# One more plain MLP chunk, wider right-operand steps, second-product loads in small pieces, its weight sums spread out, and the last steps row tile by row tile

## Chip, cores and metric

The kernel runs on 1 core of one Trainium2 chip. The metric is the device time of one execution in microseconds (us); the time before is the median of three runs. The profile is of one such execution.

## The reference

One decoder block on x of 1024 rows by 1024 columns, all in float32: sliding-window attention and a diagonal state-space branch beside each other, merged by gates, then a squared-ReLU MLP. The change touches the MLP alone:

```python
    h = rmsnorm(x, norm_mlp_pre[l])
    f = jnp.square(jax.nn.relu(h @ w_ff_in[l])) @ w_ff_out[l]   # 1024 -> 4096 -> 1024
    x = x + rmsnorm(f, norm_mlp_post[l])
```

## The kernel before

Every float32 operand of a matmul is split into a high part (rounded to the float32r type) by a ScalarE copy and a low part by a VectorE subtraction, and a product is three matmuls: high x high, high x low, low x high (`mm3`, lines 170 to 176). So the MLP keeps ScalarE and VectorE busy with splits while TensorE multiplies.

`mlp` (line 1322) makes the 4096 hidden columns in NC = 16 chunks of 256. The first N_WHOLE = 3 are plain: four products of 24 matmuls of 128x512, 96 a chunk, in halves over the rows (h = 0, 1) and the chunk's two column pieces (m = 0, 1). Chunks 0 and 1 run first their halves h = 0 and then their halves h = 1. The other chunks use Winograd's form of Strassen's scheme on a 2 x 2 blocking: seven products of 12 matmuls, 84 a chunk, with sums of blocks on both sides. The sums of the right operand, which serve all those chunks, are made by `ff1_rhs` (line 1260): T1, T2, T4 in tiles of their own, and T3 written over the block B[0, 1] of the normalised input. It is a generator in `self.side`, of which `tick` plays so many steps after each half product (`tick(9)` at 4 a step), and `drain` (line 190) plays what is left before the Winograd chunks begin. T4 is the third of three tiles from the pool `b16`, which holds seven buffers of 16 KB a partition; the buffer it gets is the one in which the second piece of weight chunk 1 is kept (`keep(self.big, (1,))`, line 217).

`units_ahead` (line 1196) feeds the Winograd chunks and the second product: a generator yields the operands one by one, `unit` (line 1185) emits the ScalarE copy at once and the VectorE low half a little later, and a ring of six buffers lets them be ahead of TensorE. `ff1_units` (line 1225) loads the raw weights of a chunk in two DMAs of 512 KB (line 1234) and makes its sums. `hid_out` (line 1310) makes four sums of a finished hidden chunk on VectorE and writes the chunk X and its sums S to `xd` in DRAM, 1 MB each (lines 1319 and 1320). All these DMAs are issued by SP's queue, which runs in order and waits at each issue until its data or its buffer are there.

The second product (`ff2`, line 1470; 4096 -> 1024) is one level of the same scheme: seven products M1, M2, M5, M6, M3, M7, M4 of 16 chunks by 4 row tiles by 3 matmuls = 192 matmuls. `ff2_units` (line 1436) yields for each chunk the left operand, read back from `xd` in pairs of chunks of 512 KB (line 1448, three buffers), and the right one, a chunk of a block of `w_ff_out` in `wb`. The blocks are loaded by `ff2_loads` (line 1425), one tile (1 MB for the first block, else 2 MB) at each of the first chunks of M1. Where the scheme wants a difference of blocks, `ff2_units` subtracts in place just ahead of the unit (lines 1457 and 1463): in M5, M6, M7 and M4. Between chunks `ff2` plays one of `steps`: copies and sums out of PSUM, in M7 the finished upper row tiles (`top`, `weigh`, `finish`: square on ScalarE with its sum, gain on POOL at line 1488, statistics, two scaled additions at line 1502, store), in M4 the preparation of the lower ones. The last four chunks of M4 run row tile by row tile; after each, `weigh` and, one tile later, `finish` follow.

What sets the order is the order of emission: each engine runs its instructions in the order in which this Python emits them, and semaphores hold them.

Of the kernel before, what the change touches and what calls it, by code (L numbers as in the profile page):

```python
# [9 lines left out]
F32 = mybir.dt.float32  # L10
# [15 lines left out]
N_WHOLE = 3  # L26
# [82 lines left out]
class Block:  # L109
# [1115 lines left out]
    def ff1_units(self, chunks):  # L1225
# [13 lines left out]
        for c in chunks:  # L1239
# [8 lines left out]
            yield self.unit(s[:, 1])  # L1248
            yield self.unit(A12)
            tt(s_[:, 0], A11, A21, ALU.subtract)  # L1250
            tt(s_[:, 1], A12, s[:, 1], ALU.subtract)
            yield self.unit(s[:, 0])
            held[0] -= 1
            load()
            yield self.unit(s_[:, 0])
            yield self.unit(s_[:, 1])
# [3 lines left out]
    def ff1_rhs(self):  # L1260
# [10 lines left out]
        def tt(o, x, y, op=ALU.subtract):  # L1271
            v.tensor_tensor(out=o, in0=x, in1=y, op=op)  # L1272
            return 4

        def put(o, k, t):
            nc.scalar.activation(out=o[0][:, k], in_=t, func=AF.Copy)
            late.append(lambda: tt(o[1][:, k], t, f(o[0][:, k])))
# [5 lines left out]
        def diff(k, x, y):  # L1283
            t, e = self.t([512]), self.t([512])
            yield tt(t, f(x[0][:, k]), f(y[0][:, k]))
            yield tt(e, f(x[1][:, k]), f(y[1][:, k]))
            yield tt(t, t, e, ALU.add)
            return t

        def less(k, x, y):  # L1290
            t = self.t([512])
            yield tt(t, f(x[0][:, k]), y)
            yield tt(t, t, f(x[1][:, k]), ALU.add)
            return t

        for k in range(4):
            t1 = yield from diff(k, B[0, 1], B[0, 0])
            put(T1, k, t1)
            t2 = yield from less(k, B[1, 1], t1)
            put(T2, k, t2)  # L1300
            yield from flush(1)
            t4 = yield from less(k, B[1, 0], t2)
            put(T4, k, t4)
            yield from flush(0)
        for k in range(4):
            t3 = yield from diff(k, B[1, 1], B[0, 1])
            put(B[0, 1], k, t3)
            yield from flush(0)
# [13 lines left out]
    def mlp(self):  # L1322
# [17 lines left out]
        for i in range(4):  # L1340
# [6 lines left out]
            for e in evacs[i]:  # L1347
                ev(ps[e], *divmod(e, 2), 0)
        self.side = [self.ff1_rhs()]
# [9 lines left out]
        for c in range(2, N_WHOLE):  # L1359
            X = self.r([4, 512])  # L1360
            pieces = [self.wq.get() for _ in range(2)]
            for h in (1, 0):
                for m in range(2):
                    for p in self.proj_halves(pieces[m], h, self.h2):
                        self.tick(9)
# [9 lines left out]
        for c in range(N_WHOLE, NC):  # L1375
# [24 lines left out]

            product("M1")
            late.append(lambda: nc.scalar.activation(out=m1, in_=ps["M1"], func=AF.Copy))
            product("M6")
            late.append(lambda: add(u, m1, ps["M6"]))
            product("M2")
            late.append(lambda: block(m1, ps["M2"], 0))
            product("M5")
            late.append(lambda: add(u5, u, ps["M5"]))
            product("M7")
            late.append(lambda: add(u7, u, ps["M7"]))  # L1410
            late.append(lambda: block(u7, ps["M5"], 3))
            product("M3")
            late.append(lambda: block(u5, ps["M3"], 2))
# [7 lines left out]
    FF2 = (("M1", (0, 0), (0, 0), None), ("M2", (0, 1), (1, 0), None), ("M5", (1, 0), (0, 0), (0, 1)),  # L1421
           ("M6", (1, 1), (0, 0), (1, 1)), ("M3", (1, 3), (1, 1), None), ("M7", (1, 2), (0, 1), (1, 1)),
           ("M4", (0, 3), (1, 0), (0, 0)))

    def ff2_loads(self):

        for j, n, pool, cs in ((0, 0, self.r, 4), (1, 0, self.big, 8), (0, 1, self.big, 8), (1, 1, self.big, 8)):
            self.wb[j, n] = []
            for c0 in range(0, NC, cs):
                t = pool([cs, 512], F32)  # L1430
                col = j * D + n * 512
# [243 lines left out]
```

## Time and profile before

| what | us |
|---|---|
| median of 3 runs | 1327.11 |
| lowest, highest run | 1324.92, 1328.24 |
| the profiled execution | 1324.95 |
| its span, first to last instruction | 1323.1 |
| TensorE busy in it | 1230.2 (93%) |
| VectorE, ScalarE, POOL busy | 888.8, 580.1, 124.6 |
| mean granted TensorE clock | 0.966 |

Times in the rows are microseconds from the span's start, durations of single instructions in a grouped row nanoseconds. PE is TensorE's matmul, PEld its weight load, DVE VectorE, ACT ScalarE, POOL GpSimd, SPq the queue that issues DMAs. L176 is line 176 of the kernel; a helper's line stands for all its callers, so the tile names tell them apart: `lo` and `hi` are the ring's unit buffers, `raw` the buffers of loads, `b`, `r`, `qp`, `t` tiles of the pools, `ps` PSUM. The part that the change touches runs from 638 us to the end.

### The profile page before, as it was taken

The page shows a single profiled execution, that of the slowest core. Times are in us where ns is not written, and L with a number is a line of the kernel's source. Part 1 is how long each engine was busy: PE and PEld are TensorE (multiplying, and loading weights), DVE is VectorE, ACT ScalarE, POOL GpSimd, SP SyncE. Part 2 cuts the span into 40 slices and gives each one's busy share as a digit, 9 for nine tenths or more (in the row PEclk, how much of TensorE's full clock was granted, in tenths as well). Part 3 has the DMA queues.
Part 4 walks back from the last instruction along what each step waited for, and adds up shares of the span by engine and source line. Part 5 has one row for each costly group of instructions (what it writes and reads, how often), then busy time and mean ns, then how long its engine had stood idle before and what let it go on. Part 6 is the DMA issues. An engine that isn't in the chain of part 4 may idle for free.

```text
span 1323.1 us, 15801 instructions
## 1 busy us (share of the span) xinstructions
PE 1230.2 (93%) x5784; PEld 1013.0 (77%) x5784; DVE 888.8 (67%) x1624; ACT 580.1 (44%) x1061; POOL 124.6 (9%) x78
## 2 busy tenths in 40 slices
PE   8999899999999999989966999999986999999795
PEld 7988788877889777768755888888864788887583
DVE  5776877645785566478597777777451476657987
ACT  4433566642114553554343555455341444444342
POOL 1000112200000033334000000000000000002212
PEclk8999899999999999999987999999998899999898
DMA  9322222298525574456042444543489222243342
GB/s 349 128 75 101 60 79 81 81 171 156 130 81 102 188 291 143 162 188 222 17 189 97 175 152 151 191 174 141 179 300 381 97 96 96 96 143 112 112 137 86
DMA packets 78749, 195.54 MB, mean 148 GB/s; under 512 B 6224, under 2 KB 23120, under 8 KB 73552
## 3 DMA queue, kind: packets, MB, share of 16 engines
q1 hardware_dynamic: 78672, 194.54, 45.1%
q8 instruction: 45, 0.74, 0.2%
q14 instruction: 32, 0.26, 0.1%
HBM read 135.30 MB, written 59.21 MB: 147 GB/s over the span
## 4 chain that ended last, share of the span: by engine, by line
PE 56%; DVE 20%; DMA 9%; ACT 8%; issue 5%; SPq 1%; POOL 1%; DVEq 0%; ACTq 0%
PE ps L175 17%; PE ps L174 17%; PE ps L176 17%; DMA raw<-xd 4%; DVE lo L158 2%; ACT r L535 2%; DVE b L164 2%; DVE t L1272 1%; DVE r L164 1%; ACT hi L156 1%; DVE lo L1193 1%; DMA raw<-in_wsb_dram 1%; DVE r L522 1%; PE ps L1157 1%; PE ps L1158 1%
## 5 line engine op out<-in xcount | busy, mean ns | idle before, releaser
L174 PE MATMUL ps<-b,hi 128*128 128x512 f32 x740 | 292.6, 395 | 1.7 <-ACT t L1039 1.3
L176 PE MATMUL ps<-b,lo 128*128 128x512 f32 x744 | 291.5, 392 | 0.9 <-DVE lo L1193 0.9
L175 PE MATMUL ps<-b,hi 128*128 128x512 f32 x740 | 289.6, 391 | 0.9 <-DVE b L164 0.9
L174 PE MATMUL ps<-lo,hi 128*128 128x512 f32 x440 | 177.1, 403 | 15.3 <-ACT lo L1192 15.3
L175 PE MATMUL ps<-lo,hi 128*128 128x512 f32 x440 | 178.0, 405 | 11.5 <-DVE lo L1193 11.4
L1193 DVE TENSOR_TENSOR hi<-raw,hi 128x512 fp32r<-128x512 f32 x128 | 90.0, 703 | 134.9 <-ACT hi L1192 134.9
L176 PE MATMUL ps<-lo,hi 128*128 128x512 f32 x440 | 175.5, 399 | 0.0
L1192 ACT ACTIVATE hi<-raw 128x512 fp32r<-128x512 f32 x128 | 80.6, 630 | 202.3 <-PE ps L176 116.2
L176 PEld LDWEIGHTS ps<-b,lo 128*128 128x128 f32 x744 | 140.7, 189 | 31.6 <-DVE lo L1193 1.6
L174 PEld LDWEIGHTS ps<-b,hi 128*128 128x128 f32 x740 | 139.6, 189 | 32.0 <-ACT t L1039 1.7
L175 PEld LDWEIGHTS ps<-b,hi 128*128 128x128 f32 x740 | 139.7, 189 | 30.0 <-DVE b L164 1.8
L158 DVE TENSOR_TENSOR lo<-raw,hi 128x1024 fp32r<-128x1024 f32 x66 | 87.9, 1336 | 82.5 <-ACT hi L156 82.1
L175 PEld LDWEIGHTS ps<-lo,hi 128*128 128x128 f32 x440 | 85.8, 195 | 35.3 <-DVE lo L1193 17.6
L174 PEld LDWEIGHTS ps<-lo,hi 128*128 128x128 f32 x440 | 85.3, 194 | 35.9 <-ACT lo L1192 17.8
L176 PEld LDWEIGHTS ps<-lo,hi 128*128 128x128 f32 x440 | 85.7, 195 | 17.7
L174 PE MATMUL ps<-b,lo 128*128 128x512 f32 x184 | 72.7, 395 | 22.7 <-ACT lo L1192 22.7
L156 ACT ACTIVATE hi<-raw 128x1024 fp32r<-128x1024 f32 x68 | 71.5, 1053 | 42.3 <-PE ps L1158 20.9
L175 PE MATMUL ps<-b,lo 128*128 128x512 f32 x184 | 72.4, 393 | 0.0
L176 PE MATMUL ps<-b,hi 128*128 128x512 f32 x180 | 70.0, 389 | 0.0
L1488 POOL TENSOR_TENSOR r<-r,qp 128x512 f32<-128x512 f32 x4 | 6.6, 1661 | 597.5 <-ACT t L1487 597.5
L1193 DVE TENSOR_TENSOR lo<-r,lo 128x512 fp32r<-128x512 f32 x73 | 50.1, 687 | 18.6 <-ACT lo L1192 18.6
L1192 ACT ACTIVATE lo<-r 128x512 fp32r<-128x512 f32 x73 | 45.4, 622 | 33.9 <-PE ps L176 32.8
(249 smaller groups left out, 2104.7 us busy)
## 6 DMA issues: line engine op xcount, KB each, us to landing
xd<-r SPq DMA_DIRECT2D x32, 1024.0 KB, 5.2
raw<-xd SPq DMA_DIRECT2D x56, 512.0 KB, 3.3
raw<-in_ff_dram SPq DMA_DIRECT2D x32, 512.0 KB, 5.7
raw<-in_win_dram SPq DMA_DIRECT2D x26, 512.0 KB, 4.5
raw<-in_wout_dram SPq DMA_DIRECT2D x24, 512.0 KB, 4.1
b<-in_ff_dram SPq DMA_DIRECT2D x6, 2048.0 KB, 16.2
r<-in_x_dram SPq DMA_DIRECT2D x14, 512.0 KB, 6.2
sd<-t SPq DMA_DIRECT2D x16, 256.0 KB, 2.0
```

The costliest lines, as they stand in the source:

```text
L156: nc.scalar.activation(out=hi, in_=src, func=AF.Copy)
L158: return (hi, lo), lambda: eng.tensor_tensor(out=lo, in0=src, in1=hi.bitcast(F32), op=ALU.subtract)
L164: (eng or nc.vector).tensor_tensor(out=lo, in0=src, in1=hi.bitcast(F32), op=ALU.subtract)
L174: self.nc.tensor.matmul(ps, lhsT=ah, rhs=bh, start=first and i == 0, stop=False)
L175: self.nc.tensor.matmul(ps, lhsT=ah, rhs=bl, start=False, stop=False)
L176: self.nc.tensor.matmul(ps, lhsT=al, rhs=bh, start=False, stop=last and i == n - 1)
L522: nc.vector.tensor_tensor_reduce(out=S[:, h - kv * G, 0:kk], in0=ps[:, gi, 0:kk], in1=self.bias[:, h, b0:256], op0=ALU.add, op1=ALU.max, s ...
L535: nc.scalar.activation(out=S[:, g, 0:kk], in_=S[:, g, 0:kk], func=AF.Exp, bias=nm[:, g:g + 1], accum_out=rs[:, g:g + 1])
L1157: nc.tensor.matmul(ac[c], lhsT=a, rhs=wl[:, cs], start=False, stop=False)
L1158: nc.tensor.matmul(ac[c], lhsT=b, rhs=wh[:, cs], start=False, stop=k == 7)
L1192: self.nc.scalar.activation(out=both[:, 0], in_=src, func=AF.Copy)
L1193: lo = lambda: self.nc.vector.tensor_tensor(out=both[:, 1], in0=src, in1=both[:, 0].bitcast(F32), op=ALU.subtract)
```

## The change

Constants: four plain chunks instead of three, and the last six chunks of M4 instead of four run row tile by row tile.

First product: the Winograd products come in the order M1, M2, M3, M5, M6, M7, M4, with u5 now M3 copied plus M5 and added to u later; the left sums of `ff1_units` stand behind the first unit. `ff1_rhs` works on 1024 columns at a time (28 steps instead of 56), its cost is 6.5 a step and a tick gives 11; T3's part waits until the last half product that reads B[0, 1] has been emitted.

Second product: `ff2_loads` goes. `ff2_jobs` gives each load (two chunks, 512 KB) and each weight difference a step, that is a chunk counted through the seven products. Eight loads of the first block come at steps 0, 0, 0, 2, 4, 6, 8, 10, the other 24 at 1.25 times their number; the differences at 24, 40, 52 and 66 plus the chunk. End: the gain is a VectorE step; sums, squares, gain, statistics and scaled additions become separate steps, `must` first and then `rest`, with two a chunk in M4; each half row is stored by itself (256 KB); of the last tiles' work the sum, square and gain of tile t stand ahead of the statistics of tile t - 1.

```diff
-N_WHOLE = 3
+N_WHOLE = 4
+TAIL = 6
...
+            yield self.unit(A11)
+            load()
             tt(s[:, 0], A21, A22, ALU.add)
             tt(s[:, 1], s[:, 0], A11, ALU.subtract)
-            yield self.unit(A11)
-            load()
...
-        for k in range(4):
-            t3 = yield from diff(k, B[1, 1], B[0, 1])
-            put(B[0, 1], k, t3)
+        while not self.b12_done:
+            yield "wait"
+        for ks in (slice(0, 2), slice(2, 4)):
+            t3 = yield from diff(ks, B[1, 1], B[0, 1])
+            put(B[0, 1], ks, t3)
             yield from flush(0)
...
             for p in self.proj_halves(first[i], 1, self.h2):
-                self.tick(9)
+                self.tick(11)
...
+        for i, (jn, c) in enumerate(itertools.product(((0, 0), (1, 0), (0, 1), (1, 1)), range(0, NC, 2))):
+            at(2 * i - 4 if i < 8 else 1.25 * i, functools.partial(load, *jn, c))
+        for c in range(NC):
+            at(24 + c, functools.partial(less, (0, 0), (0, 1), (0, 0), c))
+            at(40 + c, functools.partial(less, (0, 0), (1, 1), (0, 0), c))
+            at(52 + c, functools.partial(less, (0, 1), (1, 1), (0, 1), c))
+            at(66 + c, functools.partial(less, (1, 0), (1, 0), (0, 0), c))
...
-        load(2)
-        for name, _, at, less in self.FF2:
+        for i, (name, _, at) in enumerate(self.FF2):
             for c in range(NC):
-                w = self.wb[at][c]
+                for job in jobs.pop(i * NC + c, ()):
+                    job()
+                if i + c == 0:
+                    load(2)
...
-            nc.gpsimd.tensor_tensor(out=f, in0=f, in1=g[:, halves[n]], op=ALU.mult)
+        def gain(f, n):
+            v.tensor_tensor(out=f, in0=f, in1=g[:, halves[n]], op=ALU.mult)
...
+        def put(t, n, f, r1):
+            xx = x1[t][:, halves[n]]
+            v.scalar_tensor_tensor(out=xx, in0=f, scalar=r1, in1=xx, op0=ALU.mult, op1=ALU.add)
+            nc.sync.dma_start(out=self.out[0, t * P:(t + 1) * P, halves[n]], in_=xx)
...
+        def top(t):
+            f = C11[:, t], C12[:, t]
+            ss = self.small(3, "ss3")
+            for n in range(2):
+                squares(f[n], ss[:, n:n + 1])
+            gain(f[0], 0)
+            yield
+            gain(f[1], 1)
+            r1 = rstd(ss)
+            yield
+            for n in range(2):
+                put(t, n, f[n], r1)
+            if t == 0:
+                load_x1(3, self.q([D]))
+            yield
...
-            end = NC - 4 if name == "M4" else NC
+            end = NC - TAIL if name == "M4" else NC
...
-                next(self.wb_loads, None)
-                for _ in range(1 + (len(steps) > 12)):
-                    if steps:
-                        steps.pop(0)()
+                for _ in range(1 + (name == "M4")):
+                    if must:
+                        must.pop(0)()
+                    else:
+                        next(rest, None)
...
+            f, ss = U[:, 0, t], ss1[:, 2 * t:2 * t + 2]
+            tt(f, f, ps["M4"][t])
+            squares(f, ss[:, 0:1])
+            gain(f, 0)
             if prev:
                 prev()
-            tt(U[:, 0, t], U[:, 0, t], ps["M4"][t])
-            weigh(U[:, 0, t], 0, ss1[:, 2 * t:2 * t + 1])
-            prev = lambda t=t: finish(4 + t, (U[:, 0, t], U[:, 1, t]), ss1[:, 2 * t:2 * t + 2])
```

## Rows read from the trace of the kernel before

**Rows 1.** The page, busy time by engine: us (share of the span) xinstructions.

```profile
PE 1230.2 (93%) x5784; PEld 1013.0 (77%) x5784; DVE 888.8 (67%) x1624; ACT 580.1 (44%) x1061; POOL 124.6 (9%) x78
```

**Rows 2.** Windows: length, busy us (instructions) of each engine, granted clock, DMA share, GB/s.

```profile
682.50:705.50 23.00, 0.41 (x2) 0.00 (x0) 19.78 (x31) 7.14 (x13) 0.00 (x0) 0.61 0.44 160
705.50:712.00 6.50, 5.52 (x13) 3.94 (x14) 6.37 (x11) 2.92 (x6) 0.00 (x0) 0.55 0.08 27
712.00:956.70 244.70, 244.70 (x1080) 202.40 (x1078) 169.94 (x268) 116.73 (x197) 0.00 (x0) 1.00 0.46 163
956.70:986.80 30.10, 28.66 (x121) 22.21 (x120) 18.42 (x30) 14.70 (x26) 0.00 (x0) 1.00 0.79 258
986.80:1072.70 85.90, 70.55 (x267) 55.12 (x266) 32.31 (x51) 29.03 (x52) 0.00 (x0) 0.88 0.61 222
1203.20:1262.70 59.50, 49.43 (x194) 38.57 (x194) 52.04 (x89) 24.69 (x52) 13.44 (x8) 0.91 0.33 116
1289.90:1300.50 10.60, 9.08 (x37) 6.37 (x36) 9.82 (x13) 5.33 (x10) 2.48 (x2) 1.00 0.18 74
1308.90:1323.10 14.20, 0.13 (x1) 0.00 (x0) 8.13 (x20) 2.03 (x6) 2.52 (x2) 0.61 0.28 111
```

**Rows 3.** Waits of TensorE from 700 us on: total us, times, longest.

```profile
PE ps L174 <- ACT lo L1192: 38.0, 6, 22.7
PE ps L175 <- DVE lo L1193: 11.4, 10, 3.1
```

**Rows 4.** Timeline of ScalarE: start, us, instruction, [idle before it <-releaser].

```profile
661.08 0.63 ACT L1276 ACTIVATE b<-t 128x512 fp32r<-128x512 f32 x1 [13.59 <-PE ps L176]
```

**Rows 5.** Timelines of VectorE and TensorE at the first Winograd chunk.

```profile
705.63 0.68 DVE L1243 TENSOR_TENSOR r<-raw 128x512 f32<-128x512 f32 x1
706.35 0.69 DVE L1243 TENSOR_TENSOR r<-r,raw 128x512 f32<-128x512 f32 x1
706.96 0.68 DVE L1193 TENSOR_TENSOR lo<-raw,lo 128x512 fp32r<-128x512 f32 x1
...
707.70 0.80 PE L176 MATMUL ps<-b,lo 128*128 128x512 f32 x1 [0.92 <-DVE lo L1193]
```

**Rows 6.** SP's timeline at a chunk border; DMA issues of 732 to 735: KB, us to landing.

```profile
732.88 0.33 SPq L1319 DMA_DIRECT2D xd<-r  x1
734.20 7.94 SPq L1234 DMA_DIRECT2D raw<-in_ff_dram  x2
...
raw<-in_ff_dram SPq DMA_DIRECT2D x1, 512.0 KB, 7.3
```

**Rows 7.** Waits, 940 to 1030; DMA issues at 984; line 1448's landings, 1040 to 1110.

```profile
ACT hi L1192 <- DMA raw<-xd: 50.6, 5, 12.7
...
raw<-xd SPq DMA_DIRECT2D x1, 512.0 KB, 15.9
...
DMA to landing us min/median/max: 3.2/3.3/4.5
```

**Rows 8.** Timelines of VectorE and POOL in M7; waits of 1205 to 1250.

```profile
1208.50 1.78 DVE L1463 TENSOR_TENSOR b<-b,b 128x512 f32<-128x512 f32 x1
1209.69 1.74 POOL L1488 TENSOR_TENSOR t<-t,qp 128x512 f32<-128x512 f32 x1
...
ACT lo L1192 <- DVE b L1463: 24.1, 9, 3.7
```

**Rows 9.** VectorE's timeline at the last row tile; DMA issues of the whole span.

```profile
1314.74 0.68 DVE L1474 TENSOR_TENSOR b<-b,ps 128x512 f32<-128x512 f32 x1
1316.27 0.21 DVE L1493 TENSOR_SCALAR m<-mx 128x1 f32<-128x1 f32 x1 [0.85 <-ACT t L1487]
1318.01 1.41 DVE L1502 SCALAR_TENSOR_TENSOR b<-b,r,b 128x512 f32<-128x512 f32 x2
...
sd<-t SPq DMA_DIRECT2D x16, 256.0 KB, 2.0
...
out_dram<-b SPq DMA_DIRECT2D x4, 512.0 KB, 2.6
```

More of the change, by code (lines that the diff above doesn't have):

```diff
@@ L1436, in ff2_units @@
     def ff2_units(self):
         nc = self.nc
-        self.wb = {}
-        self.wb_loads = self.ff2_loads()
-        next(self.wb_loads)
-        raws = [(blk, c) for _, blk, _, _ in self.FF2 for c in range(0, NC, 2)]
+        self.wb, self.wb_tiles = {}, {}
+        jobs = self.ff2_jobs()
+        raws = [(blk, c) for _, blk, _ in self.FF2 for c in range(0, NC, 2)]
         loaded = []
@@ L1499, in finish @@
             v.tensor_tensor(out=r1, in0=r0, in1=e, op=ALU.mult)
-            for n in (1, 0):
-                ns = halves[n]
-                v.scalar_tensor_tensor(out=xx[:, ns], in0=f[n], scalar=r1, in1=xx[:, ns], op0=ALU.mult, op1=ALU.add)
-            nc.sync.dma_start(out=self.out[0, t * P:(t + 1) * P, :], in_=xx)
-        def top(t, ss):
-            f1 = self.t([512])
-            tt(f1, U[:, 0, t], U[:, 1, t])
-            tt(f1, f1, ps["M3"][t])
-            weigh(C11[:, t], 0, ss[:, 0:1])
-            weigh(f1, 1, ss[:, 1:2])
-            return lambda: finish(t, (C11[:, t], f1), ss)
+            return r1
+        def put(t, n, f, r1):
[17 more added lines that the diff above has]
+            yield
         ss1 = self.small(NH, "mx")
         ps = {}
-        for name, _, _, _ in self.FF2:
-            steps = list(late)
+        rest = iter(())
+        for name, _, _ in self.FF2:
+            must = list(late)
             late.clear()
-            each = lambda f: steps.extend(functools.partial(f, t) for t in range(4))
+            each = lambda f: must.extend(functools.partial(f, t) for t in range(4))
             if name == "M2":
@@ L1531, in ff2 @@
             if name == "M7":
-                for t in range(4):
-                    ss = self.small(3, "ss3")
-                    done = []
-                    steps += [lambda t=t, ss=ss, done=done: done.append(top(t, ss)), lambda done=done: done[0]()]
-                    if t == 0:
-                        steps.append(lambda: load_x1(3, self.q([D])))
+                C12 = self.big([4, 512], F32)
+                each(lambda t: tt(C12[:, t], U[:, 0, t], U[:, 1, t]))
+                each(lambda t: tt(C12[:, t], C12[:, t], ps["M3"][t]))
+                x1b = self.big([4, D], F32)
+                must.append(lambda: [load_x1(4 + t, x1b[:, t]) for t in range(4)])
+                rest = itertools.chain(*(top(t) for t in range(4)))
             if name == "M4":
-                x1b = self.big([4, D], F32)
                 each(lambda t: tt(U[:, 0, t], U[:, 0, t], ps["M7"][t]))
-                each(lambda t: tt(U[:, 1, t], U[:, 0, t], U[:, 1, t]))
-                each(lambda t: weigh(U[:, 1, t], 1, ss1[:, 2 * t + 1:2 * t + 2]))
-                each(lambda t: load_x1(4 + t, x1b[:, t]))
+                each(lambda t: (tt(U[:, 1, t], U[:, 0, t], U[:, 1, t]), squares(U[:, 1, t], ss1[:, 2 * t + 1:2 * t + 2])))
+                each(lambda t: gain(U[:, 1, t], 1))
             ps[name] = [self.ps() for _ in range(4)]
@@ L1556, in ff2 @@
                 make()
-                next(self.wb_loads, None)
-                for _ in range(1 + (len(steps) > 12)):
-                    if steps:
-                        steps.pop(0)()
-            for step in steps:
+                for _ in range(1 + (name == "M4")):
[3 more added lines that the diff above has]
+                        next(rest, None)
+            for step in must:
                 step()
+        for _ in rest:
+            pass
         aw = [(c, get(), get()) for c in range(end, NC)]
```

117 lines of the change are left out of this document (64 added, 53 removed).

## The prediction

> **What bounds the kernel now.** TensorE is busy for 93% of the span [rows 1], so I looked first for the stretches where it is not, and asked for the busy times of the MLP in windows cut at those places [rows 2]. The reader is to see one clean window and several broken ones. From 712 to 956.7 us, 1080 matmuls take 244.7 us: one each 0.2266 us at full clock, nothing lost. That price times the matmuls that a window must run, taken from its length, gives what the window loses (the counts in the rows include one to three that straddle an edge; I use the program's numbers, 192 for a product of the second matrix):
> - 682.5 to 712: 29.5 us for 13 matmuls, **26.5 lost**.
> - 956.7 to 986.8: 30.1 for 120, **2.9 lost**; 986.8 to 1072.7: 85.9 for 264, **26.1 lost**.
> - 1203.2 to 1262.7: 59.5 for 192, **16.0 lost**.
> - 1289.9 (end of chunk 9 of the last product M4) to the end at 1323.1: **33.2 us**, of which 14.2 follow the last matmul.
>
> The granted clock is below 1.00 in all of these but the first 30 us of the second product and the stretch before 1308.9 (0.55 to 0.91), and the losses contain that. Next the waits of TensorE [rows 3]: 38.0 us on ScalarE's unit copies (22.7 once, 15.3 in five others) and 11.4 on VectorE's low halves. What stood behind each comes from the timelines and the DMA views [rows 4 to 9], in the parts below.
>
> **The extra plain chunk and the wide steps.** The 26.5 us are `drain()`: VectorE still works at `ff1_rhs` when the three plain chunks end. It was late because ScalarE's copy into T4 sat 13.59 us until 661.1 [rows 4]: T4's buffer is the one that holds a weight piece until then. The fourth plain chunk is 96 matmuls in place of 84, so 12 x 0.2266 = **+2.7 us** of TensorE, and 21.8 us of cover. VectorE owes 28 wide steps; two narrow ones start 0.61 apart [rows 5], so a wide one is about 1.2. The ninth stands behind T4's copy, so some nine are done by 661; 19 x 1.2 = 23 plus three `hid_out` (2.5 each) and three weight splits (1.2 each) makes 34 us, due by 704.3, 43 us later. So the steps hide, even though T3's eight wait for `b12_done` and have the last half chunk (10.9 us) for about 10 us of work.
>
> But a new thing is late: **the first raw weights of the Winograd chunks**. `ff1_units` issues them only after `hid_out(3)` on SP, whose first issue waits for the last matmul's two ScalarE passes. Count from the last plain matmul: 1.7 us to that issue (0.4 of matmul end, two passes of 0.63 as in [rows 4]); the same three issues stand at a chunk border, where the raw follows the first xd write by 1.32 us and lands 7.3 us later behind 2 MB of writes [rows 6]. So A11 lands at 10.3, is copied by 10.9, the first two matmuls go. VectorE's two sums now stand ahead of A11's low half and need the second raw, issued 1.2 us after the first: they start at 11.5, and sum, sum, low half took 2.0 us (705.63 to 707.64 [rows 5]); the third matmul goes at 13.5, as it went at 707.70 before. Less 0.7 of useful matmuls, plus some 2 us of low clock as the rows after 705.5 show, **14.9 lost instead of 26.5: -11.6**. Bounds: 5 if the loads came at once, 26.5 if nothing were covered.
>
> **Order inside the Winograd chunks** (M1, M2, M3, M5, M6, M7, M4): one more ScalarE copy, the same VectorE adds. TensorE loses nothing there now and VectorE is busy 170 of 245 us, so 0.
>
> **Second product's loads.** The 26.1 us are four waits of ScalarE on raw xd reads: 50.6 us in five waits, 12.7 the longest (that one sits ahead of the product) [rows 7]. These 512 KB reads landed after 15.9 us, against 3.3 in undisturbed products [rows 7], because 15 of the 16 MB of `wb` went out within nine chunks. Now 13 pieces of 0.5 MB and 8 raws go out in M1: 11 MB in 43.5 us is 253 GB/s, no more than the 258 moved up to 986.8, with 2.9 lost, and the 222 after it, over twice the time [rows 2], and each piece is issued four chunks (10.9 us) before its use. On SP each stands behind a raw whose buffer VectorE must free, at most a chunk or so; that leaves twice the 3.3 us. **26.1 goes to about 0.5: -25.6.** Ahead of the first raw, three pieces (1.5 MB) replace one of 1 MB: at 258 GB/s 0.5 MB is 2.0 us; the ring of units is empty there, so it shows, less a little that VectorE's own backlog hides: **+1.6**. The bounds are 0 and +3, and 0 to 12 for loads that remain late.
>
> **Weight sums spread out, gains on VectorE.** In M7 VectorE was busy 52 of 59.5 us: low halves, 16 sums, the four finished row tiles, all in that product. POOL's gain of 1.74 us stretched a VectorE step from 0.68 to 1.78, and ScalarE waited 24.1 us for the sums [rows 8]. Now M7's 16 sums run in M6 and M3 and M4's 16 in M3 (two of them in M7), and the gain is one VectorE step of 0.68. The busiest earlier product, M6, then holds 32 low halves and 20 sums, 52 x 0.61 = 32 us of 43.5; M7 holds 32 low halves, 2 sums, 8 adds and 2 1/3 row tiles (some 6 us each): 42 x 0.61 + 14 = 40. A gain waits for ScalarE's square, itself behind the unit copies; that delays VectorE by at most one chunk of the three that the ring holds. **16.0 goes to 0.5: -15.5**; bounds -16 and -8.
>
> **The last steps.** Call E the end of chunk 9 of M4. Before, E to end was 33.2. The row tiles that are left (5 of 12 steps) fall in chunks 6 to 8: gains 3 x 0.7, two statistics chains of 1.74 [rows 9] with ScalarE's root behind unit copies, four puts of 0.7. Chained through, VectorE is free for chunk 10's low halves only at E+1 and for the six last chunks' at E+8.6, so row tile 0 ends at E+9.3, not E+4.1. Then per tile: add to statistics 1.53 [rows 9], in which the gain waits for the square, gain 0.65, chain without POOL about 1.45, puts 1.35: 5.0 us against 4.1 of matmuls, first two tiles without backlog. Ends: E+11.6, 18.5, 23.6, 28.6, last chain and puts 31.4. Then 3.7 us from 1319.4 to the span's end, less 0.6 as a 256 KB store lands in 2.0 and a 512 KB one in 2.6 [rows 9]: 34.5, with 0.7 for a possible low clock 35.2: **+2.0**. So row-tile order gains nothing: VectorE sets this end before and after. Bounds -3 and +9 (the tiles at half clock).
>
> **Sum**, against the profiled execution (1324.95, its span 1323.1 and 1.85 around it): -11.6 + 2.7 - 25.6 + 1.6 - 15.5 + 2.0 = -46.4, so 1278.5. The median of the three runs lies 2.2 above the profiled one; I carry most of that and say **1280**.
>
> **Rivals.**
> - The raws arrive earlier or VectorE's order doesn't matter: only 5 lost at the border, 1270. For: an undisturbed read lands in 3.3 [rows 7]. Against: SP is in order, and the 2 MB lie ahead. Chance 0.15.
> - What is covered is only partly so: leftover `ff1_rhs` (up to +11.6), M1's loads half late (+12), or the last tiles at half clock (+7); one of them gives 1287 to 1296. For: VectorE idles until 661 whatever is emitted, and the last product is crowded. Against: the slack counted above. That the extra chunk covers nothing at all is 1292, within this. Chance 0.23.
> - Slower than before: small pieces don't overlap, each holds the path for its whole landing. By their steps M1 and M2 carry 13 pieces and 8 raws each, M5 6 and 8: 21 x 3.3 [rows 7] = 69 us twice and 14 x 3.3 = 46, in place of 43.5 each: +54, 1334. It decides from 2.1 us of path for each transfer in M1. Against: at 258 GB/s [rows 2] a piece is 2.0 us of path, and two or more were in flight then. Chance 0.04.
> - The rule behind that rival: the Trainium skill, "DMA: Bandwidth & Descriptors", section Bandwidth, asks for transfers of 1 MiB and more, as smaller ones waste the path, and so speaks against cutting 2 MB loads into 0.5 MB. By that rule the time is nearer to 1334, by the rows 1280: a 0.5 MB read took 3.3 us by itself and 15.9 behind two 2 MB loads [rows 7], so here it is the large ones that hold the path, and I give the rule no more than that chance.
>
> **How the numbers follow.** Forecast 0.58 (1272 to 1287), earlier border 0.15, partial cover 0.23, slower 0.04. The range 1264 to 1295 leaves out about two in ten. About 0.3%, 4 us, is what a measurement of this kernel can tell from no change. Only the serial rival, and a little of mishaps that I don't see, reaches it: faster 0.94, same 0.02, slower 0.04.
>
> **What would show it.** In the changed profile: a hole of 10 to 14 us after the last plain matmul that ends with a raw's landing, with `ff1_rhs` done before it (right), or with VectorE in `ff1_rhs` (wrong); no ScalarE wait on raw<-xd above 1 us in M1's second half; raws landing under 8 us; M7 at 43.5 to 45 us; VectorE late at the last six chunks, then its chain of adds and puts to the end. The prediction is wrong if the border closes in 5 us, or if M5 and M6 show new waits on `wb` loads.

## The result, and the profile after

The changed kernel takes 1278.38 us (median of four runs, 1276.39 to 1281.95) against 1326.01 (1322.52 to 1328.24) for the kernel before in the same comparison: a ratio of 0.965, 95% interval 0.961 to 0.968. Forecast were 1280 and 1264 to 1295. The profiled execution took 1276.67 us with a span of 1274.9; the one of before had 1324.95 and 1323.1, so the spans differ by 48.2.

The page's busy times, which answer to [rows 1]: TensorE does 12 matmuls more and is 95% busy instead of 93%, VectorE has 28 instructions fewer.

```profile
PE 1216.6 (95%) x5796; PEld 1007.3 (79%) x5796; DVE 871.9 (68%) x1596; ACT 581.1 (46%) x1059; POOL 99.8 (8%) x62
```

The windows of the changed kernel that answer to [rows 2], with the same columns (start and end, length, busy time and count of PE, PEld, DVE, ACT and POOL, granted clock, DMA share, GB/s): the last plain chunks, the border, the Winograd chunks, M1 and M2, M7, the end up to about the last matmuls, and what follows them.

```profile
638.00:703.70 65.70, 65.45 (x287) 53.97 (x288) 47.12 (x48) 28.81 (x42) 0.00 (x0) 1.00 0.26 104
703.70:724.00 20.30, 7.43 (x22) 5.15 (x21) 8.81 (x13) 6.14 (x10) 0.00 (x0) 0.66 0.58 207
724.00:948.10 224.10, 224.10 (x990) 185.34 (x988) 153.43 (x242) 110.64 (x188) 0.00 (x0) 1.00 0.45 162
949.30:1040.00 90.70, 89.57 (x385) 73.17 (x386) 55.92 (x89) 44.78 (x79) 0.00 (x0) 0.98 0.79 268
1170.50:1214.10 43.60, 43.60 (x194) 36.08 (x194) 30.76 (x58) 21.51 (x42) 0.00 (x0) 1.00 0.48 169
1241.30:1261.40 20.10, 17.35 (x70) 12.49 (x69) 14.55 (x29) 6.20 (x16) 0.00 (x0) 1.00 0.14 53
1261.40:1274.90 13.50, 0.87 (x4) 0.38 (x2) 8.23 (x25) 1.57 (x5) 0.00 (x0) 0.62 0.32 117
```

The reader is to see that M7 has become a clean window (43.6 us for 192 matmuls, clock 1.00) where it took 59.5, that M1 and M2 together now need 90.7 us where they took 30.1 + 85.9, and that the one long broken window left ahead of the end is the 20.3 us at the border.

Below, "lost" is the time from one matmul's start to the next over 0.227 us, added up over a stretch of the trace. E is, as in the prediction, the end of chunk 9 of M4. One term of the sum is not lost time: the 12 matmuls.

| stretch | lost before | lost after | change | forecast |
|---|---|---|---|---|
| border before the Winograd chunks | 26.3 | 15.7 | -10.7 | -11.6 |
| 12 more matmuls | | | +2.7 | +2.7 |
| M1 and M2, with the first units of M1 | 29.0 | 4.9 | -24.2 | -25.6 + 1.6 |
| M7 | 15.9 | 0.0 | -15.9 | -15.5 |
| E to the end of the span (all of it) | 33.2 | 33.6 | +0.4 | +2.0 |
| up to the start of the part that the change touches | | | -0.5 | 0 |
| sum | | | -48.2 | -46.4 |

M5, M6 and M3 lose nothing in either kernel. The last line but one is not the change's doing: in the executions told of below this part (it begins with the halves h = 1 of chunks 0 and 1, at 638.5 before and 638.0 after) starts anywhere from 636.8 to 641.5 us, whatever was edited. So single executions are compared here by what a stretch loses, and not by their totals alone.

**The border.** The timeline of TensorE, VectorE, ScalarE and SP in the changed kernel (start, duration, instruction, idle time before it and what ended it), and the landing of the loads that SP issues from 706.51 on (count, KB, median us from issue to landing):

```profile
703.71 0.39 PE L177 MATMUL ps<-b,lo 128*128 128x512 f32 x1
715.49 0.79 PE L175 MATMUL ps<-b,lo 128*128 128x512 f32 x1 [11.39 <-ACT lo L1193]
718.19 0.80 PE L177 MATMUL ps<-b,lo 128*128 128x512 f32 x1 [1.48 <-DVE lo L1194]
...
706.37 1.23 DVE L1273 TENSOR_TENSOR b<-r,b 128x1024 fp32r<-128x1024 f32 x1 [0.25 <-ACT b L1277]
716.11 0.69 DVE L1244 TENSOR_TENSOR r<-raw 128x512 f32<-128x512 f32 x1 [8.52 <-DMA raw<-in_ff_dram]
...
714.81 0.63 ACT L1193 ACTIVATE lo<-raw 128x512 fp32r<-128x512 f32 x1 [8.47 <-DMA raw<-in_ff_dram]
...
705.42 0.32 SPq L1322 DMA_DIRECT2D xd<-r  x1
706.14 0.32 SPq L1323 DMA_DIRECT2D xd<-r  x1
706.51 3.79 SPq L1235 DMA_DIRECT2D raw<-in_ff_dram  x3
...
raw<-in_ff_dram SPq DMA_DIRECT2D x3, 512.0 KB, 8.3
```

The last step of `ff1_rhs` (L1273) is done at 707.6, and then VectorE and ScalarE both stand still for 8.5 us until the raw weights land: what the prediction called the new late thing.

**The end.** VectorE's timeline of the last row tiles, which answers to [rows 9]: the four additions of a finished tile into the sum (L1497), one gain between them, and the last pair of scaled additions.

```profile
1250.02 0.69 DVE L1497 TENSOR_TENSOR b<-b,ps 128x512 f32<-128x512 f32 x1 [0.83 <-PE ps L177]
...
1258.98 0.68 DVE L1497 TENSOR_TENSOR b<-b,ps 128x512 f32<-128x512 f32 x1
1260.45 0.69 DVE L1512 TENSOR_TENSOR b<-b,qp 128x512 f32<-128x512 f32 x1 [0.79 <-ACT t L1509]
1263.86 0.68 DVE L1497 TENSOR_TENSOR b<-b,ps 128x512 f32<-128x512 f32 x1
...
1270.26 1.41 DVE L1527 SCALAR_TENSOR_TENSOR b<-b,r,b 128x512 f32<-128x512 f32 x2
```

### The profile page after: what moved, and what is told of

It reads as the page before. It is cut to its first block, busy times and chain, and to the rows that moved or that the text cites. A ratio compares the mean times of both kernels' runs of the same rounds, so it can differ in the third digit from the quotient of the medians.

```text
span 1274.9 us, 15769 instructions
## 1 busy us (share of the span) xinstructions
PE 1216.6 (95%) x5796; PEld 1007.3 (79%) x5796; DVE 871.9 (68%) x1596; ACT 581.1 (46%) x1059; POOL 99.8 (8%) x62
## 4 chain that ended last, share of the span: by engine, by line
PE 66%; DVE 16%; ACT 8%; DMA 5%; issue 4%; SPq 1%; POOL 0%; DVEq 0%; ACTq 0%
PE ps L175 20%; PE ps L176 20%; PE ps L177 20%; DVE lo L159 2%; ACT r L536 2%; DVE b L165 2%; DVE r L165 1%; DVE r L523 1%; ACT hi L157 1%; DMA raw<-in_ff_dram 1%; PE ps L1158 1%; PE ps L1159 1%; PE ps L1157 1%; DMA raw<-in_win_dram 1%; DMA r<-ud 1%
## 5 line engine op out<-in xcount | busy, mean ns | idle before, releaser
L175 PE MATMUL ps<-b,hi 128*128 128x512 f32 x760 | 300.1, 395 | 1.7 <-ACT t L1040 1.3
L177 PE MATMUL ps<-b,lo 128*128 128x512 f32 x760 | 297.4, 391 | 1.5 <-DVE lo L1194 1.5
L176 PE MATMUL ps<-b,hi 128*128 128x512 f32 x760 | 296.9, 391 | 0.9 <-DVE b L165 0.9
L176 PE MATMUL ps<-hi,lo 128*128 128x512 f32 x432 | 169.2, 392 | 2.9 <-DVE hi L1194 2.9
L175 PE MATMUL ps<-hi,lo 128*128 128x512 f32 x432 | 168.9, 391 | 1.1 <-ACT hi L1193 1.1
L175 PEld LDWEIGHTS ps<-b,hi 128*128 128x128 f32 x760 | 143.2, 188 | 32.9 <-ACT t L1040 1.8
L177 PE MATMUL ps<-hi,lo 128*128 128x512 f32 x432 | 168.9, 391 | 0.0
L176 PEld LDWEIGHTS ps<-b,hi 128*128 128x128 f32 x760 | 143.3, 189 | 30.6 <-DVE b L165 1.8
L1193 ACT ACTIVATE lo<-raw 128x512 fp32r<-128x512 f32 x126 | 79.5, 631 | 183.1 <-PE ps L177 152.2
L1194 DVE TENSOR_TENSOR lo<-raw,lo 128x512 fp32r<-128x512 f32 x126 | 87.1, 691 | 89.5 <-ACT lo L1193 89.2
L176 PEld LDWEIGHTS ps<-hi,lo 128*128 128x128 f32 x432 | 81.5, 189 | 21.5 <-DVE hi L1194 4.8
L175 PEld LDWEIGHTS ps<-hi,lo 128*128 128x128 f32 x432 | 81.5, 189 | 18.5 <-ACT hi L1193 1.5
L177 PEld LDWEIGHTS ps<-hi,lo 128*128 128x128 f32 x432 | 81.4, 188 | 17.0
L175 PE MATMUL ps<-b,lo 128*128 128x512 f32 x168 | 66.5, 396 | 11.4 <-ACT lo L1193 11.4
L176 PE MATMUL ps<-b,lo 128*128 128x512 f32 x168 | 66.1, 394 | 0.0
L177 PE MATMUL ps<-b,hi 128*128 128x512 f32 x168 | 65.4, 389 | 0.0
L1194 DVE TENSOR_TENSOR hi<-r,hi 128x512 fp32r<-128x512 f32 x72 | 49.5, 687 | 22.4 <-ACT hi L1193 22.4
L1193 ACT ACTIVATE hi<-r 128x512 fp32r<-128x512 f32 x72 | 44.7, 621 | 35.5 <-PE ps L177 35.5
L1158 PE MATMUL ps<-lo,b 128*128 128x512 f32 x128 | 51.0, 399 | 5.5 <-DVE lo L159 5.3
```

The costliest lines, as they stand in the source:

```text
L175: self.nc.tensor.matmul(ps, lhsT=ah, rhs=bh, start=first and i == 0, stop=False)
L176: self.nc.tensor.matmul(ps, lhsT=ah, rhs=bl, start=False, stop=False)
L177: self.nc.tensor.matmul(ps, lhsT=al, rhs=bh, start=False, stop=last and i == n - 1)
L1158: nc.tensor.matmul(ac[c], lhsT=a, rhs=wl[:, cs], start=False, stop=False)
L1193: self.nc.scalar.activation(out=both[:, 0], in_=src, func=AF.Copy)
L1194: lo = lambda: self.nc.vector.tensor_tensor(out=both[:, 1], in0=src, in1=both[:, 0].bitcast(F32), op=ALU.subtract)
```

## Experiments

The labels with r are edits of the changed kernel, those with b of the kernel before. Where no ratio is given, the number is of one execution.

**The first raw loads ahead of the last stores.** Theory: the hole at the border is SP's order alone. Rival: VectorE's or ScalarE's backlog sets it.

```diff
         load()
+        yield
         for c in chunks:
...
+        units = self.ff1_units(range(N_WHOLE, NC))
         for c in range(2, N_WHOLE):
             X = self.r([4, 512])
             pieces = [self.wq.get() for _ in range(2)]
+            if c == N_WHOLE - 1:
+                next(units)
...
-        make, get = self.units_ahead(itertools.chain(self.ff1_units(range(N_WHOLE, NC)), self.ff2_units()))
+        make, get = self.units_ahead(itertools.chain(units, self.ff2_units()))
```

> The changed kernel with one thing moved: the first three raw loads of the Winograd chunks are issued when the fourth plain chunk begins, ahead of its hid_out on SP's queue. Theory (the hole of 11.8 us at the border is the landing of these loads, held by SP's order): the hole ends when ScalarE has finished the last evacuation and T3's copy, 3.3 us after the last plain matmul, and the third matmul goes some 5.8 us after it instead of 14.5; the border loses 6 to 8 us instead of 15.7, the execution takes 8 to 10 us less than the changed kernel's 1276.7, so about 1268. Rival (the hole is VectorE's and ScalarE's remaining steps of ff1_rhs, and the loads only end last by a little): 0 to 3 us less.

Measured: 1270.09 us (1267.83 to 1271.35) against 1323.69 for the kernel before beside it, ratio 0.960 (0.958 to 0.962). TensorE at the border:

```profile
702.83 0.39 PE L177 MATMUL ps<-b,lo 128*128 128x512 f32 x1
706.03 0.50 PE L175 MATMUL ps<-b,lo 128*128 128x512 f32 x1 [2.81 <-ACT lo L1193]
708.71 0.79 PE L177 MATMUL ps<-b,lo 128*128 128x512 f32 x1 [1.94 <-DVE lo L1194]
```

The hole is 3.2 us from start to start instead of 11.8, the third matmul comes 5.9 us after the last plain one instead of 14.5, and the border loses 7.9 instead of 15.7. SP now issues these loads at 684.8 us, 18 us before the last plain matmul, so the order on SP was the cause. ScalarE's two passes over the last product and T3's copy (703.3 to 705.5) hold what is left of the hole, and VectorE's last step of `ff1_rhs` with the two left sums what is left ahead of the third matmul.

**Three plain chunks again.** How much is the extra chunk worth in the changed kernel?

```diff
-N_WHOLE = 4
+N_WHOLE = 3
```

> The changed kernel with three plain chunks again, all else kept. Theory (with the raw loads behind hid_out, the border's hole is the larger of leftover ff1_rhs and the loads): VectorE ends hid_out(2) about 9 us after the last plain matmul, the loads land some 8 us later, the border loses about 21 us instead of 15.7, and 12 matmuls (2.7 us) are saved: 2 to 4 us more than the changed kernel, about 1279. Rival (the extra chunk is what takes the old loss away): the loss of 26 us is back, 8 us more.

Measured: 1278.69 us, 2.0 above the profiled execution of the changed kernel. SP's timeline at the border, and the waits between 681 and 702 us (total, times, longest):

```profile
685.24 0.32 SPq L1322 DMA_DIRECT2D xd<-r  x1
690.34 0.32 SPq L1323 DMA_DIRECT2D xd<-r  x1
690.71 2.46 SPq L1235 DMA_DIRECT2D raw<-in_ff_dram  x3
...
PE ps L175 <- ACT lo L1193: 15.4, 1, 15.4
ACT lo L1193 <- DMA raw<-in_ff_dram: 8.2, 1, 8.2
```

Without the extra chunk the hole is 15.8 us and the border loses 20.0, 4.3 more than with it; the 12 matmuls cost 2.7 of that. The sums that the second store writes stand behind steps of `ff1_rhs` on VectorE (four wide ones from 682.95 on) and end at 690.3, so that store is 5 us behind the first one, not 0.7 as in the changed kernel, and the raw loads behind it on SP with it. So, as the kernel stands, the chunk brings some 2 us (4.3 - 2.7 at the border, 0.5 in M1): most of its cover goes to waiting for a load that nothing but its place in the queue holds back.

With three plain chunks as before, this border still loses 6.3 less than in the kernel before. VectorE ends `ff1_rhs` 9.6 us after the last plain matmul (691.5 against 681.9), before 23.2 (705.7 against 682.5). VectorE's idle time around T4's copy, in the kernel before and in this run, shows where it gained:

```profile
662.90 0.69 DVE L1314 TENSOR_TENSOR r<-r 128x512 f32<-128x512 f32 x1 [12.13 <-ACT r L1331]
...
661.63 1.23 DVE L1273 TENSOR_TENSOR b<-r,b 128x1024 fp32r<-128x1024 f32 x1 [4.51 <-ACT b L1277]
```

Ahead of that idle time VectorE has done nine steps of `ff1_rhs` in both, but here each is twice as wide.

**Narrow steps again.** Are the wide steps of `ff1_rhs` worth anything?

```diff
-            return 6.5
+            return 4
...
-        for ks in (slice(0, 2), slice(2, 4)):
+        for ks in (slice(k, k + 1) for k in range(4)):
...
-                self.tick(11)
+                self.tick(9)
```

> The changed kernel with the steps of ff1_rhs 512 columns wide again (56 steps at 4, a tick gives 9), the wait for the last reader of B[0, 1] kept. Seven of T3's 16 steps are then left for the drain, some 6 us of VectorE after the last plain matmul, while the raw loads land 11 us after it: by my account the border loses 15.7 us as with wide steps, the execution changes by less than 2 us. Rival (the wide steps are what lets ff1_rhs end in time): the border loses 3 us more or above.

Measured: 1275.87 us; the border loses 15.5 against 15.7. They are worth nothing that shows here, since `ff1_rhs` ends before the raw weights land either way: with narrow steps its last one ends at 711.4 us and the first Winograd matmul starts at 714.6.

This and the run before take out the chunk and the wide steps one at a time, each with the other in place, and in a kernel whose border waits for the loads either way. No run takes out both, nor either of them once the loads are moved. There the wide steps could show: `ff1_rhs` ends 3.9 us after the last plain matmul with them (707.6 against 703.7) and 8.4 without (711.4 against 702.9). So 2 us and nothing are what each is worth beside the other, and not what they would be worth alone.

**Large loads at the spread times, and small loads early.** The prediction set the small pieces against a rule of the Trainium skill that asks for large ones. The change did two things at once, size and time, and these two runs take them apart. First, 2 MB (for the first block 1 MB) in one transfer at the step of its first piece; then the 0.5 MB pieces at about the times of the kernel before.

```diff
         def load(j, n, c):
...
-            self.nc.sync.dma_start(out=t[:, i:i + 2], in_=self.I["ff2"][c:c + 2, :, col:col + 512].rearrange("c p x -> p c x"))
+                col = j * D + n * 512
+                self.nc.sync.dma_start(out=t, in_=self.I["ff2"][c:c + cs, :, col:col + 512].rearrange("c p x -> p c x"))
```

> The changed kernel, but each tile of the second product's right operand loaded whole (1 or 2 MB in one DMA) at the step of its first piece, so large loads spread out as the small ones are. Theory A (what cost 26 us before was that nearly all loads went out within nine chunks): no change beyond 2 us, M1 and M2 of the second product lose about 5 us as now. Theory B (large transfers hold the path whenever they run, small pieces are the cure): waits on raw reads come back at each of the seven 2 MB or 1 MB loads, 10 to 25 us more.

```diff
-            at(2 * i - 4 if i < 8 else 1.25 * i, functools.partial(load, *jn, c))
+            at((0, 0, 3, 3, 4, 4, 5, 5)[i] if i < 8 else 6 + (i - 8) // 4, functools.partial(load, *jn, c))
```

> The changed kernel with its small pieces of 0.5 MB, but issued as early as before: the first block's at steps 0 to 5, the other 24 at four a step from step 6 to 11. Theory A (timing is the cause): the path is again full for some 40 us, raw reads land after 10 us or more, 15 to 25 us more than the changed kernel. Theory B (size is the cause): no change beyond 2 us.

Measured: 1277.28 us with large loads spread out, 1301.36 with small loads early. M1 and M2 lose 5.8 in the first, 27.8 in the second, 4.9 in the changed kernel and 29.0 before. The windows of M1 and M2 with large loads, then with small early ones, and of each the landings of its DMAs (count, KB, us from issue) from 949 to 1000 and from 960 to 1010; last the wait of ScalarE in the second (total, times, longest):

```profile
949.80:1040.50 90.70, 89.69 (x385) 72.96 (x386) 55.91 (x89) 44.79 (x79) 0.00 (x0) 0.98 0.72 261
...
raw<-xd SPq DMA_DIRECT2D x9, 512.0 KB, 5.0
b<-in_ff_dram SPq DMA_DIRECT2D x2, 2048.0 KB, 10.0
```

```profile
949.90:1064.70 114.80, 97.43 (x385) 75.94 (x384) 55.09 (x88) 44.23 (x79) 0.00 (x0) 0.93 0.66 234
...
b<-in_ff_dram SPq DMA_DIRECT2D x24, 512.0 KB, 10.8
raw<-xd SPq DMA_DIRECT2D x7, 512.0 KB, 10.8
...
ACT lo L1193 <- DMA raw<-xd: 49.1, 5, 12.1
```

The early small pieces bring back the picture of [rows 7] almost to the number (50.6 us in five waits there, 49.1 in five here), the spread large ones don't. The time of issue is the cause; the size is not, as it moves M1 by 0.9 us, and in favour of the small pieces. The Trainium skill, "DMA: Bandwidth & Descriptors", section Bandwidth, asks to batch transfers to 1 MiB or more; with 2 MB and with 0.5 MB loads the windows of M1 and M2 take the same 90.7 us and move 261 and 268 GB/s, so its rule decides nothing here.

**M7: sums back, gain back on POOL, and both.** The prediction said that VectorE had too much to do in M7. Theory A: the total of VectorE, stretched by POOL, is what decides, so both together bring back 4 to 10 us. Rivals: the sums alone, or POOL's gains alone, made the old loss.

```diff
-            at(66 + c, functools.partial(less, (1, 0), (1, 0), (0, 0), c))
+            at(80 + c, functools.partial(less, (1, 0), (1, 0), (0, 0), c))
```

> The changed kernel with M4's weight sums in M7 (steps 80 to 95) instead of 66 to 81, so M7 holds 14 sums more. VectorE is busy 30.8 of M7's 43.6 us in the changed kernel's rows; 14 sums at 0.61 make 39.4. Theory A (M7's old loss of 16 us needs VectorE full, from sums and POOL's gains together): M7 loses 0 to 2 us. Theory B (the sums alone were the cause; my prediction's estimate of 40 us plus 8.5 makes 48): M7 loses 4 to 8 us.

```diff
-            v.tensor_tensor(out=f, in0=f, in1=g[:, halves[n]], op=ALU.mult)
+            nc.gpsimd.tensor_tensor(out=f, in0=f, in1=g[:, halves[n]], op=ALU.mult)
```

> The changed kernel with the gain on POOL again, sums spread out as they are. Theory A: M7 and M4's first part have room for VectorE steps that POOL stretches by 1.1 us each, so M7 loses 0 to 2 us; in the last row tiles the gain leaves VectorE's chain and runs beside it, and the end comes 0 to 3 us earlier than the 33.6 us after chunk 9 of M4. Theory B (POOL's hold on VectorE alone made the old loss): M7 loses 5 us or more.

Both edits together:

> Both of the two: M4's sums in M7 and the gain on POOL. By theory A VectorE has 39.4 us of work less 5 gains (3) plus about ten stretched steps (11) = 47 in 43.6: M7 loses 4 to 10 us, clock included, although neither part alone loses 3. If each alone loses its share already, the parts add instead.

Measured: 1278.65, 1278.23 and 1280.97 us, and M7 loses 0.0 in all three. The last one's higher total is no effect of it: the part that the change touches starts at 641.5 in it, the latest of all. Its M7 window, and VectorE and POOL when their steps meet:

```profile
1174.70:1218.20 43.50, 43.50 (x193) 36.02 (x192) 38.16 (x68) 21.36 (x42) 6.68 (x4) 1.00 0.48 169
...
1203.92 1.29 POOL L1512 TENSOR_TENSOR r<-r,qp 128x512 f32<-128x512 f32 x1 [568.95 <-DMA b<-x1d]
1203.96 1.81 DVE L1451 TENSOR_TENSOR b<-b,r 128x512 f32<-128x512 f32 x1
1205.17 1.74 POOL L1512 TENSOR_TENSOR b<-b,qp 128x512 f32<-128x512 f32 x1
1211.56 0.68 DVE L1451 TENSOR_TENSOR b<-b,r 128x512 f32<-128x512 f32 x1
1212.14 2.46 POOL L1512 TENSOR_TENSOR r<-r,qp 128x512 f32<-128x512 f32 x1 [5.23 <-ACT t L1509]
1212.17 0.68 DVE L1194 TENSOR_TENSOR lo<-raw,lo 128x512 fp32r<-128x512 f32 x1
```

The sums are back, the stretching is back (a VectorE step of 1.81, as the 1.78 of [rows 8]), VectorE is busy 38.2 of 43.5 us, and TensorE loses nothing. Theory A's forecast misses, but the full VectorE that it needs (47 us by its sum) did not come about, so the theory isn't decided by this run. The two rivals get no support: neither the sums nor the gains bring back any loss here. Also, moving the gain off POOL brought nothing at the end: E to the end is 33.5 with the gain on POOL, 33.6 with it on VectorE.

**The same from the other side, in the kernel before.** First its gain on VectorE alone, then its sums alone, worked out earlier as in the change (the in-line differences go, and at the start of each chunk those of `(24, (0,0), (0,1), (0,0))`, `(40, (0,0), (1,1), (0,0))`, `(52, (0,1), (1,1), (0,1))` and `(66, (1,0), (1,0), (0,0))` that are due are run). Theory C: the sums cost time only where they stand directly ahead of the unit that uses them. Rivals: POOL's hold on VectorE (P), or four whole row tiles in one product (T).

```diff
-            nc.gpsimd.tensor_tensor(out=f, in0=f, in1=g[:, halves[n]], op=ALU.mult)
+            v.tensor_tensor(out=f, in0=f, in1=g[:, halves[n]], op=ALU.mult)
```

> The kernel before with one part of the change: the gain of the finished row tiles on VectorE instead of POOL. Since neither POOL's gains nor M4's sums in M7 nor both bring a loss back in the changed kernel, what took away M7's old loss of 15.9 us is open. Theory C (coupling: a sum stands just ahead of its unit, so ScalarE's copy waits for VectorE's sum while VectorE's row-tile steps wait for ScalarE, and neither can run ahead): M7 still loses 8 us or more. Theory P (POOL's hold on VectorE): M7 loses 3 us or less. Theory T (four whole row tiles with 56 steps in one product are too many): M7 still loses 8 us or more, here and with the sums moved.

```diff
+                for first, o, x, y in (...):
+                    if 0 <= i * NC + c - first < NC:
+                        sub(o, x, y, i * NC + c - first)
...
-                    nc.vector.tensor_tensor(out=w, in0=w, in1=self.wb[less][c], op=ALU.subtract)
...
-                elif less:
-                    nc.vector.tensor_tensor(out=w, in0=self.wb[less][c], in1=w, op=ALU.subtract)
```

> The kernel before with one part of the change: the four sets of weight sums at steps 24, 40, 52 and 66 plus the chunk, ahead of their units, loads and row tiles as before. Theory C: M7 loses 2 us or less. Theory P: the gains still stretch VectorE, M7 loses 8 us or more. Theory T: M7 loses 8 us or more. M1 and M2 keep their 29 us in every theory.

Measured: 1328.28 us with the gain on VectorE, M7 losing 14.9 and E to the end 38.0; 1312.43 with the sums spread, M7 losing 5.7 and E to the end 30.6. The windows of M7, the first with ScalarE's wait for the sums:

```profile
1202.90:1261.30 58.40, 47.24 (x194) 36.66 (x193) 49.81 (x97) 24.54 (x52) 0.00 (x0) 0.97 0.33 118
...
ACT lo L1192 <- DVE b L1463: 24.3, 10, 3.7
```

```profile
1203.60:1252.90 49.30, 45.99 (x194) 36.91 (x193) 38.55 (x72) 24.04 (x52) 13.00 (x8) 0.97 0.40 139
```

POOL is not the main cause: with no POOL work at all M7 loses 14.9 instead of 15.9, and ScalarE waits 24.3 us for the sums, as the 24.1 of [rows 8]. With the sums worked out earlier 10.2 of the 15.9 us go. But that edit does two things: the sums no longer stand directly ahead of their units, and M7 holds 13.5 us less for VectorE, 38.55 instead of the 52.04 of [rows 2]. VectorE's old total is more than the 43.5 us that M7's matmuls take, by some 6 us even with no POOL beside it (49.81). No run keeps the total and moves the sums, or the reverse; which of the two is worth how much of the 10.2 stays open.

What is left is between C, which expected at most 2 us to stay, and T, which expected 8 or more: 5.7 stay, with VectorE busy 38.55 of 49.3 us. The same 38 us of VectorE work cost nothing in the changed kernel, so VectorE's total is not what holds these 5.7. The four upper row tiles lie otherwise in M7: before in a few long steps, all four in M7, after in many short ones, of which fewer fall into M7. Which of these does it, and whether POOL has a share there (13.0 us of work against 6.7), was not taken apart and stays open. (E to the end shortens too, by 2.6 us, as M4's sums no longer stand in M4.)

**A shorter tail.** Four chunks row tile by row tile instead of six.

```diff
-TAIL = 6
+TAIL = 4
```

> The changed kernel with the last four chunks of M4 row tile by row tile instead of six. My prediction held that VectorE's chain sets the end before and after, so row-tile order gains nothing: row tile 0 then ends at about the same time (9.0 us after chunk 9 against 8.8), each further tile takes VectorE's 4.9 us, the first without waiting for 4.1 us of matmuls: the end comes 0 to 2 us earlier than now (33.6 us after chunk 9). Rival (six chunks a tile hide the work of the tiles behind matmuls): 2 to 5 us later.

Measured: 1277.13 us. The window from E:

```profile
1243.05:1275.30 32.25, 16.78 (x73) 13.25 (x71) 22.81 (x53) 8.46 (x20) 0.00 (x0) 0.82 0.22 82
```

E to the end is 32.3 instead of 33.6, and M4 loses 0.5 instead of 4.5. VectorE's work is the same (22.81 us against 22.78 for the two windows of after), but with six chunks the low halves of all six stand in one lump ahead of the first tile, and TensorE waits for them.

**What the runs point to, together.** Raw loads first; TAIL of 4; the two raw `xd` loads ahead of the first pieces of the second product; and the gain behind the previous tile's statistics, so that VectorE doesn't wait for the square.

```diff
             for c in range(NC):
+                if i + c == 0:
+                    load(2)
                 for job in jobs.pop(i * NC + c, ()):
                     job()
-                if i + c == 0:
-                    load(2)
...
             squares(f, ss[:, 0:1])
-            gain(f, 0)
             if prev:
                 prev()
+            gain(f, 0)
```

> The changed kernel with four edits: the Winograd chunks' first raw loads at the beginning of the fourth plain chunk (worth 8.8 us of span by itself); the second product's first two raw reads ahead of the three pieces (each piece 1.3 us: the first raw lands some 4 us earlier, M1 loses 2 us instead of 4.9); the last row tiles' gain behind the statistics of the tile before, so that VectorE doesn't wait for the square (0.8 us a tile), and four last chunks instead of six: the end comes 30 to 31 us after chunk 9 instead of 33.6. Sum: 14 to 15 us less than the changed kernel, about 1263. If the VectorE chain is not what sets the end, the last 3 us don't come.

Measured: 1263.62 us (1262.84 to 1265.0) against 1325.56 for the kernel before, ratio 0.954 (0.951 to 0.957). The windows of the border, of M1 and M2, and from E to the end:

```profile
704.20:724.00 19.80, 15.05 (x54) 11.59 (x53) 12.60 (x19) 9.54 (x16) 0.00 (x0) 0.83 0.42 159
940.90:1029.50 88.60, 87.73 (x386) 71.91 (x385) 55.04 (x87) 43.09 (x77) 0.00 (x0) 1.00 0.81 276
1230.70:1261.80 31.10, 16.84 (x73) 13.25 (x72) 22.59 (x54) 8.15 (x20) 0.00 (x0) 0.84 0.23 85
```

The border loses 7.8, M1 1.5 instead of 4.9, and E to the end takes 31.1 instead of 33.6. It beats both kernels: 14.8 us below the median of the changed one.

## Why the prediction was right, and where its steps were not

The total was right to 1.6 us against the median, and each term was within 1.6 of what came. The steps were not all right.

- **The border: mechanism shown, size off by 0.9.** The hole was forecast to end with a raw's landing after `ff1_rhs` is done, and it does; moving the loads takes it from 11.8 to 3.2 us. The first issue came 1.7 us after the last matmul, as the prediction counted from [rows 4]. The mis-sized term is the landing: 7.3 us in [rows 6], 8.3 here, which moved the third matmul from 13.5 to 14.5.
- **The extra chunk as cover: right in effect, thin in worth.** It hides `ff1_rhs`, but three chunks would have done nearly as well (2.0 us). The prediction's own numbers held this: without the chunk its 43 us up to 704.3 shrink to some 21, for some 30 us of work, so VectorE would be about 9 late (an estimate from its terms; 9.6 in the run with three chunks), where it was 23 before. It didn't ask what fewer chunks would cost, and so credited the chunk with what the wait on SP then took back and with what the wide steps do when the chunk is missing.
- **The second product's loads: right.** M2 lost 0.0 and all of M1's loss lies ahead of it and in its first 15 us: 4.9 against 5.0 forecast (2.9 + 1.6 + 0.5). The raw reads landed in about 4 us, as these rows show (the last wait of ScalarE on them that is longer than 1 us is the one ahead of the product; landings from 949 to 1040). Both runs on size and time support the reason given, that nearly all loads went out within nine chunks; they do not support the remark under the rivals that it is the large loads that hold the path, as spread out these cost 0.9 us.

```profile
ACT lo L1193 <- DMA raw<-xd: 13.7, 1, 13.7
...
raw<-xd SPq DMA_DIRECT2D x17, 512.0 KB, 4.1
b<-in_ff_dram SPq DMA_DIRECT2D x21, 512.0 KB, 6.1
```

- **M7: the number right, the reason in part wrong, in part not shown.** The part that fails is POOL's stretching as a cause: with the gain on VectorE in the kernel before, 14.9 of the 15.9 us stay. Its reading of [rows 8] was off too: the VectorE step of 1.78 at 1208.50 began while POOL ran another gain, the one in the line below; the gain of 1.74 began 1.2 us after it. The other part, that VectorE had too much to do in M7, is neither shown nor refuted: it had 49.81 us of work there without any POOL beside it, and taking the sums out brings back 10.2 us, but that took away their place directly ahead of the copies as well. 5.7 us have no shown cause. The size was off: VectorE's forecast of 40 us busy was 30.8, and the changed kernel carries 38 without loss.

```profile
1208.07 1.66 POOL L1488 TENSOR_TENSOR r<-r,qp 128x512 f32<-128x512 f32 x1 [576.12 <-ACT t L1487]
```

- **The end: +0.4 instead of +2.0.** VectorE sets the end before and after, as forecast. Row tile 0's addition came at E + 8.8 (9.3 forecast), the tiles then 4.88 apart (1258.98 and 1263.86; 5.0 forecast), VectorE's end at E + 30.4 (31.4). The 0.7 for a possible low clock was not needed: the granted clock is 1.00 until about the last matmuls (1261.4). The prediction's "row-tile order gains nothing" holds for six chunks; with four chunks and the gain moved, 2.5 us are there to be had.
- **The rivals.** Raws arriving earlier, at 1270, is not what the change did, but it is what moving the first loads makes of it: 1270.09. Partial cover and serial small transfers didn't come: 26 pieces of 0.5 MB (21 of them into `b`, 5 of the first block into `r`) and 17 raw reads went out from 949 to 1040, a read every 2.1 us with landings of 4 to 6.5, so two or three were in flight at a time.

## What to carry to other kernels

When a stage ends with stores and the next begins with loads on one in-order queue, issue the next stage's first loads ahead of those stores: here a load that needed nothing waited for stores that needed the last matmul, and moving it was worth some four times what the extra chunk meant to cover the gap brought beside it. Spread prefetches to the rate at which they are used before you think of their size, and work out an operand some chunks ahead of the instruction that reads it, in a stretch where its engine has room: that was worth 10 us in M7. Where two edits cover the same gap, each looks worth little beside the other: take out both before you call one of them useless. And the busy time of an engine does not tell whether it is the limit: VectorE was busy 38 us in two runs of M7, and one lost 5.7 us, the other nothing.

## What the runs showed of the hardware

- With the small loads issued early, the 0.5 MB reads took 10.8 us to land (median), the raw reads among them no less than the pieces; spread out, raw reads took 4.1 and pieces 6.1. On this one queue a read that is needed soon gets no preference over those issued for later.
- VectorE and POOL hold each other up both ways. In the rows of both edits together, POOL's gain of 1.29 us starts at 1203.92 and the VectorE step that starts 0.04 later takes 1.81 instead of 0.68, the difference being nearly POOL's whole length. At 1212.14 it is POOL's step that takes 2.46 instead of 1.29: VectorE is in a step since 1211.56, and its next ones keep their 0.68. The Trainium skill, "SBUF — State Buffer", section "SBUF: two separate sides", describes the port pair that the two share as an exclusive lock, held for a whole instruction by whichever starts first. The first pair of rows agrees with that to 0.2 us; in the second VectorE, which was first, goes ahead with more than one instruction, so the rule gives who waits there and not for how long. In the changed kernel it cost nothing that could be measured.
